# Attention scores from one float32 copy of q and k instead of rounded parts and rests

## The chip, the cores and the metric

The kernel runs on one core of a Trainium2 chip. A core has TensorE (PE, matrix products, fed by weight loads, PEld), VectorE (DVE), ScalarE (ACT), GpSimd (POOL) and SyncE (SP), which here issues all transfers. The metric is the device time of one execution in microseconds (us); lower is better.

## The reference: two mixer layers, of which the attentions matter here

256 tokens with 1024 channels pass two layers. Each one normalises and modulates its input, multiplies it by a wide weight matrix, lets two kinds of heads work on the columns, multiplies by an output matrix and adds a gated, normalised result to the residual. Layer 0 has a state space model (SSD) and 16 attention heads (MoBA; with 256 tokens and blocks of 256 it is plain causal attention); layer 1 has 24 heads of forgetting attention and a diagonal state space model (S5). Cut to the steps that the change touches:

```python
# layer 0, heads of 64 channels: causal softmax attention
s = jnp.einsum('bhqd,bhqjpd->bhqjp', qc, kg).astype(jnp.float32) * scale
s = jnp.where(mask, s, -jnp.inf)
p = jax.nn.softmax(...)
# layer 1
s = jnp.einsum('bhqd,bhsd->bhqs', qc, kh).astype(jnp.float32) * scale
s = s + Fc[..., None] - F[:, :, None, :]
s = jnp.where(posc[:, None] >= kpos[None, :], s, -jnp.inf)
p = jax.nn.softmax(s, axis=-1)
return jnp.einsum('bhqs,bhsd->bhqd', p.astype(vh.dtype), vh)
```

## The kernel before, in words

Everything is float32. A product of two large operands is made of three products of rounded operands (`float32r`, which TensorE takes in a single pass): rounded part by rounded part, rounded part by rest, rest by rounded part. The weights stream in by units of 128 x 2048 words (`raw`). ScalarE rounds half a unit (`whi<-raw`), and VectorE or GpSimd makes the rest (`wlo<-raw,whi`). The modulated input lies in the same two parts, `hhi` and `hlo`.

**Attention.** One unit of weights gives q and k of two heads: `proj_cm` makes 48 products into one bank of PSUM (tag `mm`, four banks), 128 rows for two heads of 64 channels, 256 columns of q and 256 of k. `qkdone` then takes the bank apart. For each head it rounds q and k on ScalarE (64 rows, 512 columns) into a buffer `q`, subtracts on VectorE to put q's rest on the other 64 rows, copies the rounded k there (a step that VectorE, ScalarE or GpSimd may take, `copy2`), and subtracts once more for k's rest, `kl`. `attention` makes the scores in two banks (tag `st`, three banks), one for each head, 128 tokens at a time against 128 or 256 keys: four products over all 128 rows (rounded q and its rest, against the rounded k twice), and four over 64 rows (rounded q against k's rest), in which the two heads lie on the two halves of the array. Then come, for each head, the minimum with mask (VectorE), exp (ScalarE), the reciprocal (VectorE), the scaling (ScalarE) and the transposes of the probabilities on TensorE (`st<-ident,b`). The product with v is in float32, with the two heads on two halves of the array's columns (`y<-b,D` in layer 0, `y<-b,A` in layer 1). There are 8 such pairs of heads in layer 0 and 12 in layer 1.

**What sets the order.** `trunk` only records steps. `Plan` gives each of them a duration from a table (or the number in `together(..)`), finds what it depends on, and lays the steps out for all engines by a search that moves deadlines at random with a fixed seed; what it finds is issued as one fixed order per engine. A step that several engines may do goes to the one that the plan holds to be free. Two engines that read one bank of PSUM count as dependent on each other (in `touch`):

```python
if sp == "PSUM" or write:
    for o, q in b.reads:
        if o is not op and (write or o.eng != op.eng) and overlap(q, r):
            op.deps[o.seq] = True
```

So ScalarE's and VectorE's reads of a bank with q and k follow one another in the order in which they are recorded. Beside the first pairs of layer 1 the S5 states are worked on (`s5_pair`): B-bar comes by a transfer (`b<-s5b`) and is cast to rounded form (`r<-b`, by any of three engines), TensorE makes the states' inputs (`st<-r,r`), VectorE scans them (`b<-s5mag,b`). The S5 tables are built on GpSimd during layer 0's attention.

Names carry buffer numbers in the order of instructions (`q_81`), and none in the profile (`q`). All instructions are recorded through one helper, so the profile gives L510 for every one.

Of the kernel before, what the change touches and what calls it, by code (L numbers as in the profile page):

```python
# [28 lines left out]
# order of loading at first, in halves of units: those of the first products (0 to 13), and those of the  # L29
# modulation of the k-tiles of their rows (14 to 29)  # L30
FIRST = (14, 15, 0, 1, 16, 17, 2, 18, 19, 3, 20, 21, 4, 5, 22, 23, 6, 7, 24, 25, 8, 9, 26, 27, 10, 11, 28, 29, 12, 13)
# units of layer 0 that a piece of the later modulation follows
ADA_AT = [("z", 1), ("z", 3), ("z", 5), ("z", 7), ("qk", 1), ("qk", 3), ("qk", 5), ("qk", 7),
          ("out", 0), ("out", 1), ("out", 2), ("out", 3)]
# units of v of layer 1 that come first
# [4 lines left out]
def stream_order():  # L40
    """Units of the weights (128 x 2048 words each) in the order in which they are used."""
    gate0, gate1 = ([("gate", l, c, kh) for c in (0, 1) for kh in (0, 1)] for l in (0, 1))
    # the first products follow the modulation of their rows, a k-tile at a time
# [43 lines left out]
#  # L87
# trunk() records the work in the order in which it would be done one step after the other. Plan finds
# what each step needs (data, and a free buffer for what it makes), gives each engine an order in which
# it waits little, and issues everything in that order; Tile adds the waits.  # L90
# [8 lines left out]
class View:  # L99
    """a buffer, or a part of one, whose place is chosen when the work is laid out"""  # L100
# [32 lines left out]
class Tag:  # L133
    """buffers of one size that take turns"""
# [8 lines left out]
class Buf:  # L143
# [4 lines left out]
    def tile(self):  # L148
        """where the buffer is; a place that changes its type is a new tile for Tile"""
        t = self.tag  # L150
        if t.make is None:
            return t.slots[self.slot]
        if self.at is None:
            dt, g = t.now[self.slot]
            if dt != self.dt:
                t.slots[self.slot] = t.make(self.slot, self.dt, g + 1)
                t.now[self.slot] = (self.dt, g + 1)
            self.at = t.slots[self.slot]
        return self.at


def region(view, space):
    """partitions and runs of elements that a view covers"""
# [48 lines left out]
class Plan:  # L212
# [4 lines left out]
    # -- recording  # L217
# [16 lines left out]
    def either(self, name, method, args, *others, **k):  # L234
        """a step that one of several engines takes, whichever is free in time"""
        self.other = others
        self.add(name, self.engines[name], method, args, k)
        self.other = ()
# [47 lines left out]
    # -- order  # L286
    def delay(self, a, b):
        """from the end of a step to the start of one that needs it"""
# [33 lines left out]
    def run(self, late, window=0.05, hold=4.0, lead=16.0, spare=4.0, gain=0.0):  # L322
# [9 lines left out]
        def tensor(t, work):  # L332
            """the tensor engine runs at half its clock until it has been busy for a window of time, and again
            after one in which it did little"""
# [23 lines left out]
        while todo:  # L358
            best = None
            for e in ENGINES:  # L360
                cand, tmin = [], 1e18
                for op in ready[e]:
# [11 lines left out]
                    for b in op.bufs:  # L374
                        if b.slot is None:
                            tag = b.tag
                            k = want.get(id(tag), 0)
                            # earlier ones of this kind come first
# [49 lines left out]
            else:  # L428
                if e == "ACT" and op.need:
# [4 lines left out]
                    # a function in several sets stays in the one that is loaded  # L434
# [18 lines left out]
    def hurried(self, late, result, chance, least, amount):  # L453
        """deadlines moved forward for the steps that the tensor engine waited for"""
# [58 lines left out]
class Together:  # L513
    """steps of one engine that are issued one right after the other"""
# [23 lines left out]
def cost(name, method, a, k, out, reads):  # L538
    """time of a step in microseconds, as the guide gives it"""
# [34 lines left out]
def trunk(ctx, tc, par, s5par, x, w, dtw, fw, postg, gateb, out):  # L574
# [19 lines left out]
    # places that hold float32 at one time and rounded parts at another  # L594
# [19 lines left out]
    def rows_of():  # L614
        """rows of SEQ elements, four to a buffer; row(i, n) is n of them, from row i of the first four on"""
# [15 lines left out]
    def either2(method, *a):  # L631
        """DVE or, where all is in SBUF, Pool"""
        plan.either("DVE", method, a, *([("POOL", None, None)] if a[1].buf.tag.space == "SBUF" else []))
# [4 lines left out]
    def copy2(o, i, pool=True):  # L638
        """a copy that DVE, ACT or, between places in SBUF, Pool does"""
# [45 lines left out]
    # products that nobody needs, for the clock of the tensor engine  # L685
# [11 lines left out]
    # the condition on every partition, as a row: sums over the rows of diagonal matrices  # L697
# [26 lines left out]
    def softplus(xb, tmps):  # L724
        """max(x, 0) + log1p(exp(-|x|)), log1p(e) = 2 atanh(e / (2 + e))"""
# [23 lines left out]
    accs = {}  # L749

    def ada_piece(l, c, kh, raw):
        """cond-weighted sum of the rows of each partition"""
# [26 lines left out]
    def modulate(l, k, halves):  # L779
        """scale and shift of a k-tile of layer l: the rows are channels, the columns multiply the condition"""  # L780
# [9 lines left out]
    # ---- stream of weights: rounded part and rest, half a unit at a time --  # L790
# [8 lines left out]
    def load(i):  # L799
        """a unit, as its two halves; the first units come in halves, those of the products in other buffers"""  # L800
# [14 lines left out]
    def modulation(i):  # L815
        """pieces of the modulation from place i of the stream on"""
# [28 lines left out]
    def next_half(kdim, spare=False):  # L845
        """the next 1024 columns of the stream that enter products; modulation on the way there"""
# [7 lines left out]
    def mm3(o, terms, first=True, last=True, **kw):  # L854
        """the three terms of a product of operands in two parts, term by term"""
# [6 lines left out]
    def by_terms(s_hi, s_lo, m_hi, m_lo, ks):  # L862
        """stationary and moving parts, as functions of k"""
        return [[(a(k), b(k)) for k in ks] for a, b in ((s_hi, m_hi), (s_hi, m_lo), (s_lo, m_hi))]

    def proj_cm(done):
        """channel-major unit: bank [channel, 2, token]; a half has 128 channels"""
# [13 lines left out]
    def proj_tm(done):  # L881
        """token-major unit: bank [token, 2, channel]; a half has 512 rows of the weights"""
# [7 lines left out]
    def proj_small(l, tag):  # L890
        """few columns: those of the rounded weights, and from 32 on those of the rests"""
# [14 lines left out]
    def make_h1(m, xn):  # L906
        """the first half of the channels is rounded straight from PSUM, while DVE works on the second"""
# [32 lines left out]
    def out_proj(l, ytile):  # L940
        """rows of out_w in order; the last four for tokens 0..127 first, so that the residual of
        those tokens is on its way while the others' products are computed"""
# [14 lines left out]
        # of layer 0, two more rows are kept, in buffers that are free between the layers  # L957
# [16 lines left out]
    def residual(l, m, acc):  # L974
        """x + gate * rmsnorm(y); for layer 0 also the normalised rows of the result"""
# [30 lines left out]
    BLK = ((slice(0, 128), 0), (slice(128, 384), 1))  # L1006

    def attention(pair, qk, v, addt, y):
        """qk: per head [its rounded q and rest of q, its rounded k twice], and the rests of k"""
        sbs = [bank("st"), bank("st")]  # L1010
        heads, kl = qk
        for t in range(2):
            with plan.together():
                for n in range(4):
                    # the products of half the rows alternate between the heads, that is the halves of the array
                    j, b = divmod(n, 2) if t == 0 else (n % 2, n // 2)
                    h = slice(64 * j, 64 * j + 64)
                    s, m = (heads[j], heads[j][:, 1]) if t == 0 else (heads[j][h], kl[h])
                    T.matmul(sbs[j][:, BLK[b][0]], s[:, 0, 128 * b:128 * b + 128], m[:, 0:128 * b + 128],
                             start=(t == 0 and b == 0), stop=(t == 1), skip_group_check=True)  # L1020
# [33 lines left out]
    def qkdone(i, vt, addt, y):  # L1054
        def done(pb):
            heads, kl = [tmp("q2", [P, 2, SEQ]) for _ in range(2)], tmp("kl", [P, SEQ])
            for j, t in enumerate(heads):
                h, o = (slice(64 * n, 64 * n + 64) for n in (j, 1 - j))
                A.activation(t[h], pb[h], AF.Copy)
                V.tensor_sub(t[o, 0, :], pb[h, 0, :], t[h, 0, :].bitcast(F32))  # L1060
                copy2(t[o, 1, :], t[h, 1, :])
                V.tensor_sub(kl[h], pb[h, 1, :], t[h, 1, :].bitcast(F32))
            attention(i, (heads, kl), vt, addt, y)
# [18 lines left out]
    def s5_prepare():  # L1082
# [15 lines left out]
        # angles theta / 2, theta, 2 theta, .. 128 theta, reduced to [-pi, pi]  # L1098
# [19 lines left out]
        # e^a - 1: 2 t / (1 - t) with t = tanh(a / 2), and exp(a) - 1 where a > 1  # L1118
# [9 lines left out]
        # real part of A minus 1, imaginary part of A  # L1128
# [18 lines left out]
        # B-bar in blocks of two groups, transposed on the tensor engine  # L1147
# [29 lines left out]
        # e^{i theta t}, t = 16 a + b, is the product of two tables of 16: over b and over 16 a  # L1177
# [34 lines left out]
    # =====================================================================  # L1212
    # layer 0
    # =====================================================================
# [20 lines left out]
    # and more of them until the first products  # L1235
# [20 lines left out]
    # xbc: causal depthwise convolution over tokens  # L1256
    def conv(i, pb):
# [3 lines left out]
        if i in RAW:  # L1261
            # a copy leaves the bank to the next products
# [13 lines left out]
    for n in range(14):  # L1276
# [4 lines left out]
        # the last products are ordered by bank  # L1281
# [15 lines left out]
    # dt = softplus(..), and a dt  # L1297
# [445 lines left out]
```

## Time and profile before

| | before |
|---|---|
| median of 3 runs | 688.84 us (688.07 to 689.96) |
| profiled execution: its span, first to last instruction (no other time of it is given) | 687.6 us |
| busy PE, DVE, POOL, ACT | 556.0, 569.0, 463.2, 356.7 us |
| mean granted TensorE clock | 0.923 |
| layer 0's pairs of heads | about 180 to 282 us |
| layer 1's pairs of heads | about 490 to 645 us |

A row of the profile gives start and duration in us, the engine, the operation, and what it writes and reads as `out<-in`; a number in brackets is the engine's idle time before it and what ended it. In groups, the number after x is a count, then follow busy us and mean ns, and after the second bar the idle time before them. Rows of waits read "engine and output, what it waited for: us in total, times, longest". In the table by windows each engine has its busy time and instructions, and PEclk is the share of full speed that TensorE was granted.

### The profile page before, as it was taken

To read this page: it belongs to the slowest core of one execution; us is meant where nothing else is said; L and a number is where in the kernel's file an instruction comes from. 1 tells how busy PE (TensorE), PEld (TensorE's weight loads), DVE (VectorE), ACT (ScalarE), POOL (GpSimd) and SP (SyncE) were. 2 spreads that over 40 slices of the span, in tenths; PEclk is the share of its full clock that TensorE was granted. 3 is DMA by queue.
4 is the path that set the end of the run, shared out by engine and by line. 5 is a ranking of instruction groups with operands and counts; after the bars stand their busy time and mean duration, and the time that the engine had idled before them with its cause. 6 is when DMAs were issued, how large, how long until landed. Compare 5 with 4: busy or idle time off the path is not lost. (4 is left out here: it accounts for less than half of the span.)

```text
span 687.6 us, 10736 instructions
## 1 busy us (share of the span) xinstructions
PE 556.0 (81%) x3884; PEld 495.3 (72%) x3884; DVE 569.0 (83%) x939; ACT 356.7 (52%) x675; POOL 463.2 (67%) x385
## 2 busy tenths in 40 slices
PE   7777975788968889697789696758769789799896
PEld 6766965688868787475689694757768678687685
DVE  7898899996957998687558998998959897897864
ACT  5233693563453977544536542522536646668642
POOL 5477756767999799999625778685637574657500
PEclk9999998998999999899999898977878987999999
DMA  8982544463435556566725347254352636544431
GB/s 330 409 308 78 184 177 169 168 237 94 160 109 177 209 215 227 204 239 229 244 93 185 130 157 242 87 191 150 100 172 61 218 115 191 199 184 154 157 118 61
DMA packets 33975, 122.60 MB, mean 178 GB/s; under 512 B 3692, under 2 KB 12548, under 8 KB 23684
## 3 DMA queue, kind: packets, MB, share of 16 engines
q1 hardware_dynamic: 33924, 121.94, 49.7%
q8 instruction: 30, 0.49, 0.3%
q14 instruction: 21, 0.17, 0.1%
HBM read 115.08 MB, written 6.84 MB: 177 GB/s over the span
## 5 line engine op out<-in xcount | busy, mean ns | idle before, releaser
L510 ACT ACTIVATE whi<-raw 128x1024 fp32r<-128x1024 f32 x124 | 129.4, 1054 | 68.8 <-PE mm L510 47.3
L510 DVE TENSOR_TENSOR wlo<-raw,whi 128x1024 fp32r<-128x1024 f32 x81 | 127.5, 1582 | 31.0 <-ACT whi L510 26.5
L510 POOL TENSOR_TENSOR wlo<-raw,whi 128x1024 fp32r<-128x1024 f32 x43 | 110.5, 2574 | 47.3 <-ACT whi L510 39.2
L510 PE MATMUL mm<-hhi,whi 128*128 128x256 f32 x664 | 99.6, 293 | 5.7 <-ACT whi L510 5.6
L510 PE MATMUL mm<-hhi,wlo 128*128 128x256 f32 x656 | 98.9, 294 | 5.1 <-POOL wlo L510 4.8
L510 PE MATMUL mm<-hlo,whi 128*128 128x256 f32 x664 | 97.0, 288 | 0.0
L510 PEld LDWEIGHTS mm<-hhi,whi 128*128 128x128 f32 x664 | 89.4, 199 | 9.0 <-ACT whi L510 7.0
L510 PEld LDWEIGHTS mm<-hhi,wlo 128*128 128x128 f32 x656 | 89.0, 200 | 7.7 <-POOL wlo L510 6.0
L510 PEld LDWEIGHTS mm<-hlo,whi 128*128 128x128 f32 x664 | 87.2, 194 | 1.2 <-issue 0.4
L510 ACT ACTIVATE b<-b,s 128x128 f32<-128x128 f32 (+1 forms) x160 | 66.1, 444 | 41.0 <-DVE s L510 40.6
L510 PE MATMUL mm<-whi,r 128*128 128x512 f32 x240 | 71.4, 408 | 3.2 <-POOL r L510 3.2
L510 POOL TENSOR_TENSOR wlo<-A,whi 128x1024 fp32r<-128x1024 f32 x14 | 41.6, 2985 | 21.6 <-ACT whi L510 21.6
L510 PEld LDWEIGHTS mm<-whi,r 128*128 128x128 f32 x240 | 45.8, 195 | 14.2 <-POOL r L510 4.1
L510 PE MATMUL mm<-wlo,r 128*128 128x512 f32 x120 | 40.5, 410 | 7.9 <-POOL wlo L510 7.9
L510 DVE CUSTOM_DVE_ANT_0 raw<-raw,condb 128x1024 f32<-128x1024 f32 x32 | 43.4, 1363 | 2.3 <-DMA raw<-in_w_dram 1.8
L510 POOL TENSOR_TENSOR b<-b,b 128x256 f32<-128x256 f32 x32 | 33.2, 1059 | 12.8 <-DVE b L510 6.2
L510 PE MATMUL st<-ident,b 128*128 128x128 f32 x120 | 20.1, 298 | 22.6 <-ACT b L510 22.6
L510 ACT ACTIVATE q<-mm 64x512 fp32r<-64x512 f32 x40 | 23.6, 590 | 27.2 <-DVE kl L510 17.8
L510 POOL TENSOR_TENSOR b<-b,tb 128x512 f32<-128x512 f32 x16 | 26.1, 1629 | 13.4 <-DVE b L510 10.9
L510 PEld LDWEIGHTS st<-ident,b 128*128 128x128 f32 x120 | 14.5, 151 | 27.8 <-ACT b L510 27.2
L510 POOL TENSOR_TENSOR tb<-ta,tb 128x256 f32<-128x256 f32 x32 | 33.8, 1055 | 1.1
L510 DVE TENSOR_TENSOR_SCAN b<-s5mag,b 128x256 f32<-128x256 f32 x32 | 33.4, 1060 | 0.1
(231 smaller groups left out, 1234.0 us busy)
## 6 DMA issues: line engine op xcount, KB each, us to landing
raw<-in_w_dram SPq DMA_DIRECT2D x80, 1024.0 KB, 4.9
raw<-in_w_dram SPq DMA_DIRECT2D x16, 512.0 KB, 8.8
A<-in_w_dram SPq DMA_DIRECT2D x14, 512.0 KB, 8.7
s5tab<-tb SPq DMA_DIRECT2D x16, 256.0 KB, 2.2
tb<-s5tab SPq DMA_DIRECT2D x16, 256.0 KB, 4.5
A<-fd SPq DMA_DIRECT2D x24, 128.0 KB, 5.8
b<-s5b SPq DMA_DIRECT2D x16, 128.0 KB
A<-fd SPq DMA_DIRECT2D x24, 64.0 KB, 6.7
```

What stands on the lines that cost most here:

```text
L510: getattr(self.engines[e], method)(*[at(v) for v in a], **{n: at(v) for n, v in k.items()})
```

## The change

`qkdone` copies the bank with q and k once, on ScalarE, as float32 into one buffer `qk` (three of these instead of four `q` and two `kl`). `attention` makes the scores in float32, four products over 64 rows, the two heads on the two row halves of the array, each writing to its own bank. The planner is told 0.72 us for the four of them, the number that it already has for the product with v.

```diff
-        """qk: per head [its rounded q and rest of q, its rounded k twice], and the rests of k"""
         sbs = [bank("st"), bank("st")]
-        heads, kl = qk
-        for t in range(2):
-            with plan.together():
-                for n in range(4):
-                    # the products of half the rows alternate between the heads, that is the halves of the array
-                    j, b = divmod(n, 2) if t == 0 else (n % 2, n // 2)
+        with plan.together(0.72):
+            for b in range(2):
+                for j in range(2):
                     h = slice(64 * j, 64 * j + 64)
-                    s, m = (heads[j], heads[j][:, 1]) if t == 0 else (heads[j][h], kl[h])
-                    T.matmul(sbs[j][:, BLK[b][0]], s[:, 0, 128 * b:128 * b + 128], m[:, 0:128 * b + 128],
-                             start=(t == 0 and b == 0), stop=(t == 1), skip_group_check=True)
+                    T.matmul(sbs[j][:, BLK[b][0]], qk[h, 0, 128 * b:128 * b + 128], qk[h, 1, 0:128 * b + 128],
+                             start=(b == 0), stop=(b == 1), skip_group_check=True)
...
     def qkdone(i, vt, addt, y):
         def done(pb):
-            heads, kl = [tmp("q2", [P, 2, SEQ]) for _ in range(2)], tmp("kl", [P, SEQ])
-            for j, t in enumerate(heads):
-                h, o = (slice(64 * n, 64 * n + 64) for n in (j, 1 - j))
-                A.activation(t[h], pb[h], AF.Copy)
-                V.tensor_sub(t[o, 0, :], pb[h, 0, :], t[h, 0, :].bitcast(F32))
-                copy2(t[o, 1, :], t[h, 1, :])
-                V.tensor_sub(kl[h], pb[h, 1, :], t[h, 1, :].bitcast(F32))
-            attention(i, (heads, kl), vt, addt, y)
+            qk = tmp("qk", [P, 2, SEQ])
+            A.activation(qk, pb, AF.Copy)
+            attention(i, qk, vt, addt, y)
         return done
...
-        "q2": (512, 4, R32), "kl": (256, 2, R32),
+        "qk": (512, 3),
```

Since the planner lays everything out anew, the order changes on every engine. Three places follow. The first is TensorE at the first pair of layer 1, before:

```order
L510 MATMUL mm_129<-hlo,whi_67 128x256 x8
L510 MATMUL st_133<-q_81 128x128
L510 MATMUL st_133<-q_81 128x256
L510 MATMUL st_134<-q_82 128x128
L510 MATMUL st_134<-q_82 128x256
L510 MATMUL st_133<-kl_85,q_81 128x128
L510 MATMUL st_134<-kl_85,q_82 128x128
L510 MATMUL st_133<-kl_85,q_81 128x256
L510 MATMUL st_134<-kl_85,q_82 128x256
L510 MATMUL mm_128<-hhi,whi_66 128x256 x8
```

The same place of TensorE in the changed kernel:

```order
L510 MATMUL mm_126<-hlo,whi_67 128x256 x8
L510 MATMUL st_131<-qk_83 128x128
L510 MATMUL st_130<-qk_83 128x128
L510 MATMUL st_131<-qk_83 128x256
L510 MATMUL st_130<-qk_83 128x256
L510 MATMUL mm_126<-hhi,wlo_72 128x256 x8
```

Eight score products in two groups became four, alternating between the two banks, with products of weights on both sides as before. The second place is VectorE at this pair, before (`ISA` is the masked minimum that follows the scores):

```order
L510 TENSOR_TENSOR q_81<-mm_131,q_81 64x256
L510 TENSOR_TENSOR D_87<-b_93,tb_114 128x512
L510 TENSOR_TENSOR kl_85<-mm_131,q_81 64x256
L510 TENSOR_TENSOR A_2_3934<-a_92,a_90 128x256
L510 TENSOR_TENSOR wlo_70<-raw_64,whi_69 128x1024
L510 SCALAR_TENSOR_TENSOR b_94<-s5mag,b_94 128x256
L510 TENSOR_TENSOR q_82<-mm_131,q_82 64x256
L510 SCALAR_TENSOR_TENSOR b_94<-s5mag,b_94 128x256
L510 TENSOR_TENSOR kl_85<-mm_131,q_82 64x256
L510 TENSOR_TENSOR D_87<-b_94,tb_113 128x512
L510 TENSOR_TENSOR wlo_72<-raw_65,whi_68 128x1024
L510 ISA b_99,s_105<-st_133,A_2_3635 128x256
```

And VectorE there in the changed kernel:

```order
L510 SCALAR_TENSOR_TENSOR b_91<-s5mag,b_91 128x256
L510 TENSOR_TENSOR D_84<-b_96,tb_110 128x512
L510 SCALAR_TENSOR_TENSOR b_91<-s5mag,b_91 128x256
L510 TENSOR_TENSOR wlo_73<-raw_64,whi_69 128x1024
L510 TENSOR_TENSOR D_84<-b_91,tb_111 128x512
L510 TENSOR_TENSOR wlo_71<-raw_64,whi_66 128x1024
L510 ISA b_94,s_103<-st_131,A_2_3543 128x256
```

The four subtractions for q and k have gone from between the scans and the weights' rests. The third place is a cast of B-bar for the S5 states (`r<-b`), which stood in ScalarE's order before:

```order
L510 ACTIVATE A_2_3769<-mm_129 128x512
L510 ACTIVATE whi_68<-raw_64 128x1024
L510 ACTIVATE r_80<-b_94 128x512
L510 ACTIVATE r_75<-A_4_3337 32x256 x2
L510 ACTIVATE r_75<-r_75 64x512
L510 ACTIVATE whi_66<-raw_64 128x1024
```

In the changed kernel such a cast stands in VectorE's order:

```order
L510 SCALAR_TENSOR_TENSOR b_90<-s5mag,b_90 128x256 x2
L510 TENSOR_TENSOR D_84<-b_90,tb_111 128x512
L510 TENSOR_TENSOR wlo_73<-raw_63,whi_69 128x1024
L510 CAST r_80<-b_91 128x512
L510 TENSOR_TENSOR r_75<-A_4_3246,r_75 32x256 x2
L510 SCALAR_TENSOR_TENSOR a_86<-A_4_3246,pt,y_132 128x256
```

It moved between the two engines: of the eight casts VectorE has one before and four now, ScalarE seven and four.

## The prediction

> **What bounds the kernel now.** I read the page first: no engine is full over the span, and the two fullest are VectorE and TensorE.
>
> ```profile
> span 687.6 us, 10736 instructions
> ...
> PE 556.0 (81%) x3884; PEld 495.3 (72%) x3884; DVE 569.0 (83%) x939; ACT 356.7 (52%) x675; POOL 463.2 (67%) x385
> ```
>
> The profile gives its execution's span alone, 687.6 us; the median of the runs is 688.84, so 1.2 us lie around the span, and I add them at the end.
>
> Then the busy times in the two stretches in which q, k and attention are worked on, 8 pairs of heads of layer 0 and 12 of layer 1:
>
> ```profile
> core 0: us, PE busy (x) PEld busy (x) DVE busy (x) ACT busy (x) POOL busy (x), PEclk, DMA share, GB/s
> 180.00:282.00 102.00, 87.78 (x661) 78.08 (x662) 84.38 (x194) 66.17 (x150) 94.11 (x116) 0.95 0.54 191
> 490.00:645.00 155.00, 130.29 (x929) 112.68 (x928) 130.47 (x268) 94.77 (x220) 91.62 (x61) 0.91 0.48 158
> ```
>
> TensorE stands idle for 14.2 us of the first (102.00 - 87.78) and 24.7 us of the second. Everything not in these 39 us is TensorE's own work, so the change can win from three things: less of that work, fewer of these waits, and a clock that is granted in full where a wait made it fall. What the waits are, I took from the views of waits (of the first window, then of the second, then of the whole span):
>
> ```profile
> PE st L510 <- ACT b L510: 8.7, 4, 4.5
> ```
> ```profile
> PE st L510 <- ACT b L510: 11.6, 11, 3.0
> ```
> ```profile
> ACT q L510 <- DVE kl L510: 17.8, 9, 6.2
> ACT r L510 <- DMA b<-s5b: 33.5, 7, 10.4
> DVE r L510 <- DMA b<-s5b: 6.7, 1, 6.7
> ```
>
> The largest wait of TensorE there is that of the transposes for the softmax (20.3 us in the two windows). Its chain runs scores, VectorE (minimum), ScalarE (exp), VectorE (reciprocal), ScalarE (scaling); it waits on two engines that at the same time split q and k of the next pair. ScalarE also stands idle 17.8 us before its q copies, because its read of the bank for the second head has to follow VectorE's two reads for the first.
>
> The groups of instructions, by form, price what goes away:
>
> ```profile
> L510 ACT ACTIVATE q<-mm 64x512 fp32r<-64x512 f32 x40 | 23.6, 590 | 27.2 <-DVE kl L510 17.8 <-PE st L510 6.8 <-PE mm L510 1.9
> L510 DVE TENSOR_TENSOR q<-mm,q 64x256 fp32r<-64x256 f32 x40 | 16.9, 422 | 6.3 <-ACT q L510 5.3
> L510 DVE TENSOR_TENSOR kl<-mm,q 64x256 fp32r<-64x256 f32 x40 | 16.8, 421 | 0.7
> L510 POOL CAST q<-q 64x256 fp32r<-64x256 f32 x15 | 7.9, 527 | 31.8 <-ACT q L510 24.4 <-issue 7.0
> L510 ACT ACTIVATE q<-q 64x256 fp32r<-64x256 f32 x19 | 7.9, 416 | 0.5
> L510 ACT ACTIVATE A<-mm 128x512 f32<-128x512 f32 x23 | 13.3, 587 | 5.9 <-PE mm L510 5.9
> L510 PE MATMUL st<-q 128*128 128x128 f32 x40 | 10.7, 267 | 6.3 <-DVE q L510 4.9 <-DVE b L510 0.9 <-ACT b L510 0.5
> ```
>
> **The change, part by part.** First the products of the scores on TensorE. The trace shows the eight rounded products of a pair where nothing holds them up, and, beside them, the nearest thing to the new ones: the four float32 products of probabilities and v, two heads on two halves of the array (by columns there, by rows in the changed kernel), with the same 768 columns in all (128 and 256 for each head).
>
> ```profile
> 492.23 1.10 PE L510 MATMUL mm<-hlo,whi 128*128 128x256 f32 x8
> 493.16 0.39 PE L510 MATMUL st<-q 128*128 128x128 f32 x2
> 497.24 0.77 PE L510 MATMUL st<-q 128*128 128x128 f32 x2 [3.69 <-DVE q L510]
> ```
> ```profile
> 520.59 0.62 PE L510 MATMUL st<-q 128*128 128x128 f32 x4
> 521.14 0.50 PE L510 MATMUL st<-kl,q 64*128 64x128 f32 x4
> 521.57 1.21 PE L510 MATMUL mm<-hlo,whi 128*128 128x256 f32 x8
> ```
> ```profile
> 540.99 1.09 PE L510 MATMUL mm<-hhi,wlo 128*128 128x256 f32 x8
> 542.01 0.87 PE L510 MATMUL y<-b,A 128*64 128x256 f32 x8
> 542.81 0.97 PE L510 MATMUL mm<-hhi,whi 128*128 128x256 f32 x6
> ```
>
> The scores hold TensorE from 520.59 to 521.57, 0.98 us. The float32 group holds it from 542.01 to 542.81, 0.80 us, though each of its four products runs as two instructions. The run of eight products ahead of it takes 1.02 us (540.99 to 542.01) where the run ahead of a score group takes 0.93 (492.23 to 493.16): the array's change of form costs 0.09 more at the entry. So the new group should cost 0.80 + 0.09 = 0.89 against 0.98, and 20 pairs save 20 x 0.09 = **1.8 us**. No row shows float32 on two row halves. Its bounds are 0.80 + 0.09 from above and, if the halves take turns, what the first rival works out. I take 0.89, because it is the row with the same type, columns and number of instructions, and because the rounded products of half the rows (st<-kl,q) get four products done in 521.57 - 521.14 = 0.43 us, less than four single runs of 0.116 (0.93 / 8).
>
> The Trainium skill ("FP8 and Floating Point Precision", section "TensorE Precision Notes") says that true float32 takes four passes through the array where a rounded operand takes one. By that rule alone the new group would be an estimated 2 x (4 x 384) column passes against 8 rounded products of at most 256, and the change would lose on TensorE. The trace agrees on the passes (two instructions for each product, twice as long each), and differs on the price, since the two heads' passes lie beside each other in the 0.80 us.
>
> Second, waits inside a score group. At 493.16 two products ran, and the next two came 4.1 us later: the second head's parts were not made yet. These rows show why; first ScalarE, then VectorE:
>
> ```profile
> 488.01 0.58 ACT L510 ACTIVATE q<-mm 64x512 fp32r<-64x512 f32 x1
> ...
> 493.85 0.59 ACT L510 ACTIVATE q<-mm 64x512 fp32r<-64x512 f32 x1 [3.24 <-DVE kl L510]
> ```
> ```profile
> 488.94 3.38 DVE L510 TENSOR_TENSOR_SCAN b<-s5mag,b 128x256 f32<-128x256 f32 x2
> 492.35 0.42 DVE L510 TENSOR_TENSOR q<-mm,q 64x256 fp32r<-64x256 f32 x1
> ...
> 493.41 0.41 DVE L510 TENSOR_TENSOR kl<-mm,q 64x256 fp32r<-64x256 f32 x1
> ...
> 496.66 0.43 DVE L510 TENSOR_TENSOR q<-mm,q 64x256 fp32r<-64x256 f32 x1
> ```
>
> The chain from ScalarE to VectorE and back, twice, is queued behind scans and weight splits. It becomes one copy of 128x512, which the rows price at 587 ns. All idle time of TensorE before st<-q products is 6.3 us; a group that waits for one copy has no inside to wait in, but 0.5 of it came from the softmax and some may move ahead of the group. I take **5.5 us** (bounds 0 and 6.3). After this wait the clock stood at half:
>
> ```profile
> 496.50:503.30 6.80, 6.06 (x26) 5.54 (x27) 6.32 (x15) 2.43 (x4) 5.32 (x4) 0.50 0.65 236
> ```
>
> At half speed 6.8 us do the work of 3.4. Half of that I put down to this wait, **1.7 us** (bounds 0 and 3.4); the rest hangs on neighbouring waits.
>
> Third, the engines' load. VectorE loses 16.9 + 16.8 = 33.7 us of subtractions. ScalarE loses 23.6 + 7.9 and gets 20 x 0.587 = 11.7, net 19.8 less. GpSimd loses 7.9. None of it is on the path by itself: it lies beside TensorE's products, and the cover stays. What it does is let the softmax steps of a pair start sooner. Of the 20.3 us that the transposes waited I take a quarter, **5 us**, since VectorE's load in the two windows falls by 33.7 / (84.38 + 130.47), 16%, and a queue shrinks somewhat more than its load. Bounds: 0 and 20.3.
>
> Fourth, what the planner does with the freed time. It gives work that several engines may do to the one that it holds to be free: of the eight casts of B-bar (r<-b) four are now in VectorE's queue, one before, and ScalarE keeps four of seven. Such a cast waits for its transfer: 33.5 us in 7 waits on ScalarE, 4.8 each, and 6.7 us for the one on VectorE. On VectorE, 83% busy, everything behind it waits too: the scans, the softmax, the weights' rests. Three more cost between 0 (the same transfers were waited for on ScalarE, and the products of the states with them) and 3 x 4.8 = 14.4. I take a third, **4.6 us**, because the products wait on either engine, and only VectorE's lost time is new.
>
> Sum: -1.8 - 5.5 - 1.7 - 5.0 + 4.6 = -9.4. From the span, 687.6 - 9.4 = 678.2; with the 1.2 around it, 679.4 us. The new buffers (three of qk) and the DMA queue add no instruction.
>
> **The rivals.** *A, slower: the row halves take turns in float32.* One pass of 256 columns costs 0.116 us (0.93 / 8); 768 columns in four passes are 12 of these, 1.39 us, plus about 0.1 of start (0.80 less half of 1.39) and the 0.09 of entry: 1.58 instead of 0.98. 20 x 0.60 = 12.0 more instead of 1.8 less, so 679.4 + 13.8 = 693 us. It turns the sign once a group costs more than 0.89 + 9.4 / 20 = 1.36 us. For it speaks that no such product is in the trace; against it, that columns overlap in float32 and rows overlap in rounded form.
>
> *D, slower: VectorE blocked by the casts.* The full 14.4 us and no gain for the softmax: 679.4 + 9.8 + 5.0 = 694 us. The 6.7 us wait on VectorE speaks for it.
>
> *B, no change: the waits only move.* The scores come sooner, but weights, GpSimd (94.11 of 102 us in the first window) and transfers set the pace; only the 1.8 us and 1.7 more are left, which the casts cancel: 687 to 690.
>
> *C, a larger gain.* Half of the transposes' waits go, the casts cost nothing, and the clock gains all: 1.8 + 6.3 + 3.4 + 10 = 21.5, so 667 us.
>
> **How the numbers follow.** The main case (672 to 686.8) gets 0.50, C 0.15, B 0.13, A 0.10, D 0.12. A difference under 0.3% (2.1 us) can't be told from none, so faster is 0.65, same 0.13, slower 0.22. The main case is the likeliest, hence 679.4. For 8 in 10 the range runs from C's 667 to 692, just short of A's and D's figures, which leaves out the slower half of those and the far end of C. Slower stays that likely, because the planner's whole order is new and any single wait of 4 to 7 us that it makes eats half of the gain.
>
> **What the profile after would show.** Step one is right if the four products (eight instructions) from one qk hold TensorE about 0.8 us, and wrong at 1.3 or more. Step two: no idle time inside a score group, and no idle 17.8 us on ScalarE before the copies. Step three: VectorE's busy time near 545 us, and the transposes' wait below 18 us. Step four: waits of VectorE for B-bar's transfers, 5 to 20 us in sum. The prediction is wrong if TensorE's waits grow elsewhere by what they lose here, above all before the states' products (st<-r,r).

## The result, and the profile after

The changed kernel takes 666.69 us (median of 4 runs, 665.79 to 668.83) against 689.40 (688.07 to 692.59) for the kernel before in the same comparison: 22.7 us less, a ratio of 0.9651 with a 95% interval of 0.9617 to 0.9684. The prediction was 679.4 us with a range of 667 to 692. The direction was right; the gain is more than twice the one forecast, and the time lies 0.3 us below the range, on the figure of rival C.

The page after, span and busy times:

```profile
span 667.1 us, 10584 instructions
...
PE 548.6 (82%) x3884; PEld 485.2 (73%) x3884; DVE 544.4 (82%) x864; ACT 334.0 (50%) x633; POOL 447.0 (67%) x363
```

VectorE's busy time fell by 24.6 us and the span by 20.5. That the two are alike is no price of VectorE's time: in `held`, below, VectorE works 29.6 us less than before (539.4 against 569.0) and the span is 14.7 us shorter (672.9). To see where the time went, I cut both traces at the same amount of TensorE's work. The stretch of layer 1's attention, from the 2100th to the 2820th product of weights, first before, then after (columns as in the prediction):

```profile
485.20:663.90 178.70, 151.27 (x1047) 130.22 (x1046) 148.28 (x293) 109.66 (x245) 100.08 (x66) 0.92 0.47 159
```
```profile
481.10:643.40 162.30, 142.47 (x1046) 120.14 (x1045) 127.16 (x245) 97.10 (x223) 79.80 (x48) 0.97 0.52 175
```

Of the 20.5 us, 4.1 were gained up to the stretch's beginning (485.2 to 481.1) and 16.4 within it (178.7 to 162.3); nothing after it. Within it TensorE's idle time fell from 27.4 to 19.8 us (178.70 - 151.27 and 162.30 - 142.47), 7.6 us. Its busy time fell by 8.8 us for one instruction less, nearly all because the granted clock rose from 0.92 to 0.97: busy time times clock is 139 us in the one and 138 in the other. The rest, about 1 us, is of the size of what the products themselves save.

The waits of TensorE in that stretch, before and after:

```profile
PE st L510 <- ACT b L510: 14.4, 12, 3.0
PE st L510 <- DVE r L510: 5.3, 1, 5.3
PE st L510 <- DVE q L510: 3.7, 1, 3.7
```
```profile
PE st L510 <- ACT b L510: 6.7, 5, 2.1
PE y L510 <- POOL D L510: 5.3, 3, 3.2
PE st L510 <- DVE r L510: 3.2, 2, 2.3
```

The wait for the softmax (transposes on ScalarE's scaling) is less than half of what it was, and in this stretch the wait within the scores is gone. In layer 0 one score group still has 3.84 us of idle time inside it, between the first head's first product and the rest (first TensorE, then VectorE):

```profile
258.57 0.49 PE L510 MATMUL st<-qk 64*128 64x128 f32 x2
262.90 1.65 PE L510 MATMUL st<-qk 64*128 64x128 f32 x6 [3.84 <-DVE b L510]
```
```profile
259.43 1.38 DVE L510 CUSTOM_DVE_ANT_0 raw<-raw,condb 128x1024 f32<-128x1024 f32 x1 [3.99 <-DMA raw<-in_w_dram]
...
262.30 1.01 DVE L510 COPY b<-st 128x384 f32<-128x384 f32 x2
```

The second head's bank was not free until VectorE had copied transposed probabilities out of it, and VectorE had waited for a transfer of weights. The new groups by form, and one score group in the timeline:

```profile
L510 PE MATMUL st<-ident,b 128*128 128x128 f32 x120 | 18.6, 288 | 15.7 <-ACT b L510 13.5 <-DVE acc L510 2.3
L510 PE MATMUL st<-qk 64*128 64x256 f32 x80 | 14.6, 420 | 0.0
L510 PE MATMUL st<-qk 64*128 64x128 f32 x80 | 12.2, 346 | 4.1 <-DVE b L510 4.1
L510 ACT ACTIVATE qk<-mm 128x512 f32<-128x512 f32 x20 | 11.7, 582 | 3.6 <-PE mm L510 3.5
```
```profile
507.76 1.09 PE L510 MATMUL mm<-hlo,whi 128*128 128x256 f32 x8
508.78 0.93 PE L510 MATMUL st<-qk 64*128 64x128 f32 x8
509.64 0.62 PE L510 MATMUL mm<-hhi,wlo 128*128 128x256 f32 x3
```

The float32 group on two row halves holds TensorE 0.86 us (508.78 to 509.64), and the run ahead of it takes 1.02 us. Of the 20 groups 14 hold it 0.85 or 0.86 us up to the next instruction, the others 1.28 us or more. The copies of q and k now wait for nothing but the products.

### The profile page after: what moved, and what is told of

Its sections match the earlier page's. It is cut to its first block, busy times and chain, and to the rows that moved or that the text cites. A ratio compares the mean times of both kernels' runs of the same rounds, so it can differ in the third digit from the quotient of the medians.

```text
span 667.1 us, 10584 instructions
## 1 busy us (share of the span) xinstructions
PE 548.6 (82%) x3884; PEld 485.2 (73%) x3884; DVE 544.4 (82%) x864; ACT 334.0 (50%) x633; POOL 447.0 (67%) x363
## 4 chain that ended last, share of the span: by engine, by line
DVE 35%; PE 22%; POOL 22%; DMA 11%; issue 6%; ACT 3%; SPq 1%; POOLq 0%; DVEq 0%; ACTq 0%
PE mm L510 17%; POOL tb L510 10%; DMA b<-s5b 7%; DVE b L510 7%; POOL ta L510 6%; DVE wlo L510 5%; DVE D L510 4%; PE st L510 4%; DVE a L510 3%; DVE A L510 3%; DVE acc L510 3%; DVE raw L510 3%; DVE acol L510 2%; DMA raw<-in_w_dram 2%; POOL A L510 2%
## 5 line engine op out<-in xcount | busy, mean ns | idle before, releaser
L510 DVE TENSOR_TENSOR wlo<-raw,whi 128x1024 fp32r<-128x1024 f32 x85 | 123.7, 1462 | 34.2 <-ACT whi L510 32.2
L510 POOL TENSOR_TENSOR wlo<-raw,whi 128x1024 fp32r<-128x1024 f32 x39 | 101.2, 2600 | 66.8 <-ACT whi L510 54.5
L510 PE MATMUL mm<-hhi,whi 128*128 128x256 f32 x664 | 96.2, 286 | 8.1 <-ACT whi L510 6.6
L510 PEld LDWEIGHTS mm<-hhi,whi 128*128 128x128 f32 x664 | 87.1, 194 | 10.8 <-ACT whi L510 7.9
L510 ACT ACTIVATE b<-b,s 128x256 f32<-128x256 f32 (+1 forms) x160 | 65.8, 445 | 43.2 <-DVE s L510 43.0
L510 PE MATMUL mm<-whi,r 128*128 128x512 f32 x240 | 68.4, 398 | 2.2 <-POOL r L510 2.2
L510 POOL TENSOR_TENSOR tb<-ta,tb 128x256 f32<-128x256 f32 x32 | 37.5, 1170 | 1.0
L510 DVE TENSOR_TENSOR_SCAN b<-s5mag,b 128x256 f32<-128x256 f32 x32 | 37.4, 1191 | 0.0
L510 POOL TENSOR_TENSOR A<-A,amask 128x768 f32<-128x768 f32 x12 | 24.6, 2058 | 18.5 <-DMA A<-fd 17.7
L510 POOL TENSOR_TENSOR s<-s,nhalf 128x1 f32<-128x1 f32 (+1 forms) x9 | 6.2, 686 | 45.8 <-DVE s L510 45.7
L510 DVE TENSOR_TENSOR r<-A,r 128x512 fp32r<-128x512 f32 (+1 forms) x28 | 33.9, 1210 | 3.4 <-ACT r L510 2.9
```

The source lines that it names most:

```text
L510: getattr(self.engines[e], method)(*[at(v) for v in a], **{n: at(v) for n, v in k.items()})
```

## The experiments

All kernels here are compared with the kernel before, whose median in those comparisons was 690.4 to 691.2 us.

**The old order kept (held).** The planner laid the changed kernel out anew, so work and order changed together. This kernel separates them: it has the changed steps, but takes engine, place and buffer of each step that both kernels have from a table of the order before.

```diff
-    plan.schedule()
+    plan.take(dict(tags, **{'ps_' + n: t for n, t in banks.items()}))
...
+        t = json.loads(zlib.decompress(base64.b85decode(ORDER)))
...
+        start = [float(r) for r in t["r"]]
```

> The changed kernel's steps, issued in the order, on the engines and in the buffers that the kernel before had (the one copy of q and k where the first rounding stood, the four float32 products where the first score group stood). If the gain of 22.7 us comes from the work that is gone, at least two thirds of it stay: 667 to 674 us. If it comes from the new order that the planner drew (a lucky one, or one that uses the freed time), it keeps only what waits inside the score groups and the chain are worth: 678 to 686 us.

Measured: 674.92 us (674.58 to 675.67), ratio 0.9759 (0.9707 to 0.9812), just above the first of the two expected ranges. So about 16 us come from the work that is gone, in an order that was made for the old steps, and some 8 us more (674.9 to 666.7) from the new order. Its transposes still wait 19.0 us, against 22.6 before and 15.7 after (held, then before):

```profile
PE 548.0 (81%) x3884; PEld 484.0 (72%) x3884; DVE 539.4 (80%) x853; ACT 333.0 (49%) x636; POOL 459.4 (68%) x370
...
L521 PE MATMUL st<-ident,b 128*128 128x128 f32 x120 | 19.3, 287 | 19.0 <-ACT b L521 18.7
```
```profile
L510 PE MATMUL st<-ident,b 128*128 128x128 f32 x120 | 20.1, 298 | 22.6 <-ACT b L510 22.6
```

What is gone is not VectorE's work alone: ScalarE's busy time fell by 23.7 us as well (356.7 to 333.0).

**VectorE's load put back on spare buffers (load, held_load).** Four subtractions per pair of heads, that nobody needs; in `load` with the changed kernel's own order, in `held_load` at the places where the old subtractions stood.

```diff
+                self.engines["DVE"].tensor_sub(self.spare[0:64, 0:256], self.spare[0:64, 256:512], self.spare[0:64, 512:768])
```

> The changed kernel in its own order, with four more subtractions of 64x256 on VectorE per pair of heads (80 in all, on spare buffers, one behind each of the next four steps of VectorE), so VectorE's old load is back without the chain between ScalarE and VectorE. If VectorE's load was what cost, 10 us or more return: 677 to 690 us. If the chain was, nearly nothing returns: 666 to 671 us.

> As held (the changed steps in the order of the kernel before, 674.9 us), with VectorE's four subtractions per pair of heads put back where they stood in that order, but on spare buffers, so nothing waits for them and no chain runs through them. If VectorE's load is what the old steps cost, 686 to 692 us, as before. If the chain between ScalarE and VectorE is, 673 to 679 us.

Measured: load 692.64 us (688.86 to 695.39), held_load 702.43 (699.3 to 705.03, ratio 1.0182, 1.0137 to 1.0227): 26 and 27.5 us more than the same kernels without. Both overshot the range, and the rows say why. These are the spare subtractions of held_load, then (from the next experiment) those that read the bank of products in PSUM, as the old ones did:

```profile
L523 DVE TENSOR_TENSOR spare<-spare 64x256 f32<-64x256 f32 x80 | 73.2, 915 | 1.0
```
```profile
L522 DVE TENSOR_TENSOR spare<-mm,zero 64x256 f32<-64x256 f32 x80 | 31.1, 416 | 2.8 <-ACT qk L522 2.0
```

With both operands in SBUF one takes 915 ns, with one in PSUM 416, where the old ones took 422. The Trainium skill ("SBUF — State Buffer", section "SBUF: two separate sides") says that a VectorE instruction with two SBUF inputs and a GpSimd instruction that reads SBUF lock each other out of a shared port. The trace agrees: in held_load 48 of the 80 took more than 450 ns (the extremes are 387 and 2590), each of the 48 began while a GpSimd instruction was running, and each ended 275 to 282 ns after that one did. One of them on VectorE, and GpSimd beside it:

```profile
602.92 2.57 DVE L523 TENSOR_TENSOR spare<-spare 64x256 f32<-64x256 f32 x1
```
```profile
602.46 2.75 POOL L526 TENSOR_TENSOR wlo<-raw,whi 128x1024 fp32r<-128x1024 f32 x1 [0.80 <-ACT whi L526]
```

Of the other 32 only 3 began beside a running GpSimd instruction. In held_load2, with one operand in PSUM, 54 of the 80 did, and none took longer than 429 ns. So these two kernels put back 58.8 us (load) and 73.2 us (held_load) instead of 33.7, and what they tell is a price: 26 / 58.8 = 0.44 and 27.5 / 73.2 = 0.38 us of span for a us of VectorE.

**The load as it was (held_load2), and the chain without the load (held_chain).** In held_load2 the spare subtractions read PSUM, at the old places; no step of the attention waits for them, only the next products into that bank. In held_chain the copy is made by halves at the places of the two roundings, and behind each VectorE copies one column, for which the next half and the scores wait. This isn't wholly free of load: the halves put 11.9 us back on ScalarE (23.6 against 11.7), the columns 6.1 on VectorE.

```diff
+                for n in range(2):
+                    V.tensor_sub(spare[h, n, :], pb[h, n, :], zero[h])
...
-            A.activation(qk, pb, AF.Copy)
+            for j in range(2):
+                h = slice(64 * j, 64 * j + 64)
+                A.activation(qk[h], pb[h], AF.Copy)
+                V.tensor_copy(qk[h, 1, 0:1], pb[h, 1, 0:1])
```

> As held (674.9 us), with VectorE's four subtractions put back at their old places once more, this time each reading its half of the bank of products as the old ones did (the spare subtractions of held_load read SBUF alone and took 73.2 us together, where the old ones took 33.7). If a us of VectorE's time costs what held_load paid for it, 27.5 / 73.2 = 0.38 us, 33.7 us cost 13 and the time is 685 to 690 us: the load explains nearly all that the old steps cost in this order. If the load costs less when GpSimd isn't in its way, 676 to 681 us, and the chain has to explain the rest.

> As held, with the old chain put back without its load: the copy of q and k by halves, at the places of the two old roundings, and behind each a copy of one column on VectorE at the place of the last subtraction for that head, for which the next half and the scores wait. If the chain is what cost, 685 to 692 us. If the load is, 673 to 679 us.

Measured: held_load2 686.72 us (684.16 to 693.24, ratio 0.9961, 0.9924 to 0.9999), held_chain 678.25 (677.8 to 678.93, ratio 0.9835, 0.9801 to 0.9869). Against held the load costs 11.8 us, and the chain 3.3 at most, since part of that can be the load that came back with it. Together with held's 674.9 that is 690.0, and the kernel before took 690.4. Both lie where they were expected if the load is what cost. With intervals of 2 to 4 us on each of these figures, the two account for the difference in this order, and leave little for the rest of ScalarE's relief and for GpSimd's. What TensorE waited for in held_chain shows the chain as such, and in held_load2 the load appears where nobody waits for it by name, in the softmax, the states and the products with v:

```profile
L521 PE MATMUL st<-qk 64*128 64x128 f32 x80 | 11.6, 325 | 4.1 <-DVE qk L521 3.8 <-ACT b L521 0.2
```
```profile
PE st L522 <- ACT r L522: 24.8, 7, 7.4
PE st L522 <- ACT b L522: 22.4, 10, 4.9
...
PE y L522 <- DVE b L522: 9.9, 7, 3.5
```

Held, without the load, has 1.0 us of idle time in the first row, and 22.1, 18.7 and 5.2 us in the other three. Most of the load's cost doesn't show as waiting, though. From held to held_load2 the profiled span grows by 14.0 us (672.9 to 686.9), and TensorE's busy time by 10.8 of them (548.0 to 558.8) for the same 3884 instructions, at a granted clock of 0.915 instead of 0.935. Whether the lower clock costs that time or only goes with it stays open: held's four runs had clocks from 0.917 to 0.935 and lay within 1.1 us of each other.

**Other draws of the order (three more seeds for each kernel).** Only the planner's seed differs.

```diff
-SEED = 221
+SEED = 1
```

> The kernel before with the planner's seed 1 instead of 221. If one drawn order differs from another by little, 684 to 695 us. If the luck of the draw makes the gain, single draws of before lie 10 us or more apart: under 680 or over 700 us.

> The changed kernel with the planner's seed 1. If the gain belongs to the change, 662 to 674 us. If seed 221 was a lucky draw for it, 678 us or more.

> The kernel before with the planner's seed 2, a third draw for it (688 with 221, 684 with 1). If draws scatter by some 5 us around 688, 680 to 696 us.

> The changed kernel with the planner's seed 2, a third draw (666.7 with 221, 680.3 with 1). If the work is worth about 14 us whatever the draw, 668 to 680 us. If 221 was a lucky draw and the change is worth little, 680 us or more.

> The kernel before with seed 3, a fourth draw (689.4, 684.0, 688.2 so far): 683 to 693 us.

> The changed kernel with seed 3, a fourth draw (666.7, 680.3, 665.8 so far): 664 to 681 us; below 675 if the change's typical gain is 15 us or more.

| seed | before | after | difference |
|---|---|---|---|
| 221 | 689.40 | 666.69 | 22.7 |
| 2 | 688.15 | 665.75 | 22.4 |
| 1 | 683.97 | 680.29 | 3.7 |
| 3 | 684.75 | 678.12 | 6.6 |
| mean | 686.6 | 672.7 | 13.9 |

The times lie 5.4 us apart before and 14.5 us after. But these are not four independent draws. The traces of the changed kernel with seeds 221 and 2 show the same sequence of operations, names and shapes on VectorE, ScalarE and GpSimd (864, 633 and 363 instructions), and one that differs in 10 of 3884 places on TensorE; those with seeds 1 and 3 differ from each other in 4 places on VectorE, 2 on ScalarE, none on GpSimd and 18 on TensorE. So the changed kernel was drawn twice, not four times: one order takes 666 to 667 us, the other 678 to 680. The kernel before has nearly one order with seeds 221 and 2 and two others with 1 and 3, all within 684 to 689. The gain was 22 to 23 us with one order and 4 to 7 with the other. Their mean of 13.9 us is near held's 14 to 16, but two orders don't fix a mean.

Of the expectations, after_s1 (680.3) fell where a lucky draw of seed 221 was to show, after_s2 (665.8) came out below its range of 668 to 680, and after_s3 (below 675 us if the typical gain is 15) was missed; before_s1 to before_s3 lie in theirs, before_s1 (684.0) on the edge. The two slow draws also show a lower granted clock, 0.911 and 0.912 (after_s1, after_s3) against 0.932 and 0.928 (after, after_s2).

**TensorE kept busy in its stalls (warm).** If half clock after stalls cost time by itself, work that fills the stalls would win it back.

```diff
+            if op.seq in fill:
+                for _ in range(16):
+                    self.engines["PE"].transpose(fill[op.seq].tile()[:, 0:P], at(self.ident), at(self.ident))
```

> The changed kernel with 16 transposes of the identity, which nobody needs, ahead of each of the eight products of S5 states (st<-r,r), in the same order otherwise; they wait for the bank alone and fill the stall ahead of the states. If windows at half clock are what stalls cost beside themselves, time at half clock falls from 91 us to under 75 and the kernel to 657 to 663 us. If TensorE's clock isn't on the path there (VectorE sets the pace of S5), 665 to 670 us; if the fill delays the products, over 670 us.

Measured: 670.22 us (669.36 to 670.63), 3.5 us more than after and not less, in the range expected if the fill delays the products; the granted clock rose only from 0.932 to 0.939. The idle time before the states' products fell from 23.7 to 15.6 us, but they were no earlier on the whole (after, then warm):

```profile
L510 PE MATMUL st<-r,r 128*128 128x256 f32 x32 | 8.2, 397 | 23.7 <-ACT r L510 17.8 <-DVE r L510 5.8
```
```profile
L512 PE MATMUL st<-ident 128*128 128x128 f32 x128 | 15.6, 275 | 0.0
L514 PE MATMUL st<-r,r 128*128 128x256 f32 x32 | 6.8, 343 | 15.6 <-ACT r L514 12.0 <-DVE r L514 3.5
```

The fill took only part of the stalls, and the condition that was set, time at half clock down from 91 us to under 75, wasn't reached: the records have a clock of half or full alone, so by its mean of 0.939 the time at half clock fell to some 82 us (2 x 0.061 x 668.3). Filling stalls so far didn't pay here. That leaves open how much of the better clock in the stretch of attention is a gain by itself and how much only goes with shorter stalls, which end there for other reasons.

**More off VectorE (pt_act), and one more buffer (na14).** In pt_act the 22 copies of transposed probabilities that VectorE makes go to ScalarE, at the same place in the order; na14 uses the space that the change frees for a buffer, and is planned anew.

```diff
+            if e == "DVE" and op.seq in self.probs:
+                e = "ACT"
```
```diff
-NA = 13
+NA = 14
```

> The changed kernel in its own order, with the 22 copies of transposed probabilities that VectorE makes (550 ns each, 11.6 us) given to ScalarE (485 ns) at the same place. If VectorE's time is still worth 0.35 us per us there (11.8 us for the 33.7 of held_load2), 11.6 us less of it give 4 us: 661 to 664 us. If ScalarE's queue holds the copies up as long, or the relief ends once VectorE isn't the fullest engine, 665 to 672 us.

> The changed kernel with a fourteenth buffer of 1024 elements in the space that the smaller buffers for q and k left, planned anew with seed 221. If buffers hold the weights or S5 back, 660 to 666 us; as one more draw of the order, 666 to 680 us.

Measured: pt_act 664.17 us (663.02 to 664.48; ratio to before 0.9604, 0.9545 to 0.9663), na14 674.61 (671.48 to 676.11). pt_act's median is 2.5 us below after's, against 4 expected at 0.35 us per us, that is 0.2 us for each of the 11.6 us of copies (just outside the 661 to 664 us expected); its runs and after's don't overlap, but they were timed in different comparisons and the intervals of the ratios do overlap, so a further gain is likely and not shown. It is the fastest kernel here. VectorE in it:

```profile
PE 542.8 (82%) x3884; PEld 479.6 (73%) x3884; DVE 529.4 (80%) x842; ACT 341.9 (52%) x655; POOL 449.2 (68%) x363
```

na14 is one more draw of the order, within the scatter of the others; nothing shows that buffers hold the kernel back.

## Why the prediction was wrong, step by step

The forecast was 9.4 us of gain, the measured one 22.7. The two terms that failed are the engines' load, which was too small by 6.8 us, and the planner's new order, which had the wrong sign and was off by 12.8. The waits inside the score groups were put too high by 3.9 us, and the products by 1.2.

- **The products of the scores: right.** Forecast 0.80 us in the array and 0.09 at the entry, 1.8 us saved. Measured 0.86 and 1.02 - 0.93 = 0.09, so 0.95 instead of 0.98: 0.6 us for 20 pairs. The halves of the rows do overlap in float32; rival A is refuted. The four passes against one show in the starts of the instructions: a float32 product of 256 columns takes two of some 0.22 us each, a rounded one 0.116 us in all.
- **Waits inside a score group: the mechanism right in part, the size too large.** Forecast 5.5 us and 1.7 for the clock. held_chain gives 3.3 us at most for the chain. I had said that a group that waits for one copy has no inside to wait in. It also waits for two banks, and one group stood idle for 3.84 us inside on the second of them; that wait, and the whole 4.1 us of idle time that the score products still have, were in none of my terms.
- **The engines' load: a step that failed.** I let VectorE's 33.7 us act on the transposes' waits alone and took a quarter of those, 5 us. Held_load2 puts the load at 11.8 us, 0.35 us for each us, and its ten runs reach from 684.2 to 693.2, so that is a rough figure. The waits that grew with it are those for the softmax, the states and the products with v, and TensorE's busy time grew more than all its waits. The quantity to start from was not one wait but VectorE's busy share, 83% as a mean and 83 and 84% in the two windows of attention.
- **What the planner does with the freed time: the step that failed by most, wrong in sign.** I charged 4.6 us for casts that moved to VectorE. Its waits for B-bar's transfers rose only from 6.7 us in one to 8.5 in three, and ScalarE's fell from 33.5 in seven to 20.4 in four:

```profile
ACT r L510 <- DMA b<-s5b: 20.4, 4, 7.2
DVE r L510 <- DMA b<-s5b: 8.5, 3, 3.2
```

  The new order as a whole gave some 8 us (held against after) instead of costing any. Rival D is refuted for this order. What in the order gives the 8 us stays open: no run takes it apart. The other order that was drawn for the changed kernel (seeds 1 and 3) is 3 to 5 us slower than held's, so the sign hangs on the draw.
- **The sum as measured:** 11.8 for the load, 3.3 for the chain, 8.2 for the order make 23.3, against 22.7; the products' 0.6 is within what held contains.
- **The range.** Its lower end was set at rival C's 667, by one wait (the transposes) and the clock. That the time fell on C's figure is luck: C has no term for the order, gives 6.3 us to the waits inside score groups where the chain gave at most 3.3, and halves the transposes' waits, which fell from 22.6 to 15.7. A spread for the planner's draw was missing altogether; I spoke of single waits of 4 to 7 us, where two orders of the changed kernel lie up to 14.5 us apart.

Of what the profile after should show, VectorE's busy time (near 545 us; 544.4) and the transposes' wait (below 18; 15.7) came as forecast, though the 545 follows from no sum that I gave (569.0 - 33.7 is 535.3). ScalarE's idle time before its copies is 3.6 us, down from 27.2. That no idle time would be left inside a score group did not come true. Ahead of the states' products it fell, from 27.7 to 23.7 us.

## What to carry to other kernels

Where the fullest engine serves every stage, price work that leaves it by the us, not by the one wait in which it is seen. Here a us put back on VectorE cost 0.35 to 0.44 us of span in three kernels; a further us taken off it, in pt_act, gave about 0.2, so the price isn't a constant. Where a planner lays out the work, the comparison of two kernels holds the draw of the order as well: time a few orders of both, or keep one order for both, before the change gets the credit, and look whether two seeds really gave two orders. A copy that puts back an engine's load has to read the memories that the old work read, or it puts back another load.

## What the runs showed of the hardware that was not expected

- A VectorE subtraction of 64x256 took 416 ns with one operand in PSUM (388 to 429), and 915 ns on the mean, up to 2590, with both in SBUF; the 48 of 80 that took over 450 ns all ended 275 to 282 ns after the GpSimd instruction that ran when they began.
- Float32 products on two row halves of the array overlap as those on two column halves do: 0.86 us against 0.80 for the same columns.
- Filling part of TensorE's stalls with 128 transposes that nobody needs raised the granted clock from 0.932 to 0.939 and didn't shorten the kernel (670.2 against 666.7 us).
